# Product 4 of each column pair on the bank of products 1, 6 and 7, and a new order of the products

## The chip, the cores and the metric

The kernel runs on one NeuronCore of a Trainium2 chip. The metric is the device time of one execution in microseconds (us), the median of several runs. In the profile, PE is TensorE's matmuls, PEld its weight loads, DVE is VectorE, ACT ScalarE, POOL GpSimd, and SP the engine whose queue issues most of the DMAs. Each engine works through its own queue in order; engines wait for each other through semaphores.

## The reference

One decoder layer on a sequence of 1024 rows of width 1024. The normalized input is multiplied by one wide weight matrix, whose columns are the inputs of two kinds of heads:

```python
h = rms_norm(x, pre_g)
z = jnp.einsum('bsd,de->bse', h, w_in)          # 1024 x 1024 times 1024 x 7184
qa, ka, va, ga, qb, kb, vb, gb, gk_low = split_columns(z)
...
oa = diff_attention(qa, ka, va, lam)             # 8 heads, causal, two softmax maps each
oa = rms_norm(oa, subln_g) * (1.0 - lam_init) * silu(ga)
ob = gla_chunked(qb, kb, vb, log_a)              # 4 heads of gated linear attention
ob = rms_norm(ob, gla_g) * silu(gb)
y = jnp.einsum('bse,ed->bsd', jnp.concatenate([oa, ob], axis=-1), w_out)
return x + rms_norm(y, post_g)
```

The change lies in the projection `z = h w_in` alone.

## The kernel before, in words

**Seven products for eight.** The projection is done in 28 column pairs of 256 columns (`pairs`, lines 169 to 179). In each, the input is cut into 2 x 2 blocks of 512 x 512 (rows by depth) and the weights into 2 x 2 blocks of 512 x 128, and the four output blocks come from seven products instead of eight, by Winograd's form of Strassen's scheme. `LEFT` (line 319) names the input block of each product n; `make_weights` (line 278) makes its weight block, partly in place in the raw weights: product 5 turns b11 into b12 - b11, 6 into b22 - b12 + b11, 7 turns b12 into b22 - b12, 4 turns b21 into b21 minus what b11 now is. Each operand is split into a high part in fp32r and a rest, so that a product is three passes (high x high, rest x high, high x rest) of four matmuls of 128 x 512: twelve matmuls. The value columns VA and VB are "wide": two pairs share a weight tile, and a product has 24 matmuls of 128 x 256.

**Banks and snapshots.** A product accumulates in one of PSUM's eight banks. `step` (line 420) says which. Product 1 opens bank x; ACT copies it to SBUF as s1 (`snap`, line 424, the copy itself in line 427). Product 6 adds to the same bank x, which is copied as s2, and product 7 adds to it again, copied as s3. Product 2 opens a bank y, 5 a bank z, 4 another bank y, and 3 adds to z. The outputs are y(2) + s1, z(5) + s3, y(4) + s3 and z(5, 3) + s2. The sum of a bank and a snapshot is a DVE add (line 440, for values lines 403 and 411); `take` (line 349) and `take_values` (line 396) then split the block into high part and rest, or gate or scale it, and store it to device memory. Banks are given out in turn from the list `free` and put back in `step` once the reads from them are issued; whoever opens or adds to a bank waits for the earlier reads of it.

**The order of work.** All matmuls and transposes are pinned to the order in which the program issues them (`mm`, `tr`, lines 116 to 120). The order of the products is a list of (pair, n) written out in lines 200 to 221. Ten products stand at its head; then each pair (two pairs together where they are wide) runs 1, 2, 5, 6, 4, 7, and the third product of the pair before comes after its product 2. The last two pairs are interleaved. `go` (line 595) walks the list: it prepares the weights of the next products up to three ahead (`prepare`, in a ring of five weight buffers, `NRING`), loads the raw weights (`fetch_raw`, line 250, four buffers of 0.5 MB, two for each pair), multiplies, and does a step of converting output weights (`wo_step`, line 580: a load of 256 KB after some products, its cast to high part and rest and their stores after others, with one buffer).

Other engines' instructions are placed in their queues by a scheduler that simulates the kernel when it is built.

**Around it.** Before the products, the input is transposed and its blocks and sums are made (lines 529 to 571); decay tables for gated linear attention (GLA) are made between products (`decay`, line 680). From product 5 of pair 12 on, GLA itself runs as a filler: `go` calls `next(fill[0])` after every product, and the generator `gla` (line 758) does a block of its matmuls in some of these calls. In each half of a head, counted from 1, the 2nd call has the scores and transposes (pa, pk), the 5th the states (kv), the 7th the outputs (gpo), the 11th the norm (ms), and eleven calls make a half. The attention and the output projection follow the products.

Of the kernel before, what the change touches and what calls it, by code (L numbers as in the profile page):

```python
# [10 lines left out]
AF = mybir.ActivationFunctionType  # L11
ALU = mybir.AluOpType
PSUM = bass.MemoryType.PSUM

P = 128
# [12 lines left out]
QSCALE = 128.0 ** -0.5  # L28
# [3 lines left out]
def hymba_kernel(  # L32
# [21 lines left out]
    act, dve, pool, pe, sp = nc.scalar, nc.vector, nc.gpsimd, nc.tensor, nc.sync  # L54

    def fp(t):
        return t.bitcast(F32)
# [50 lines left out]
    free = list(range(8))  # L108
# [77 lines left out]
    def load_raw(p, halves=(0, 1)):  # L186
        if p >= len(pairs):
            return
        c0 = pairs[p][2]
        for kh in halves:  # L190
            if kh not in raws.setdefault(p, {}):
                r = ap.tile([P, HB, 256], F32, tag="raw", name="w_raw", bufs=4)
                rows = slice(kh * 512, kh * 512 + 512)
                sp.dma_start(r, w_in[0, rows, c0 : c0 + 256].rearrange("(k p) c -> p k c", p=P))
                raws[p][kh] = r
# [3 lines left out]
    EARLY = 5  # L199
    order = [(0, 1), (1, 1), (0, 2), (1, 2), (2, 1), (3, 1), (2, 2), (3, 2), (4, 1), (4, 2)]  # L200
    n_early = len(order)
    y, z = len(pairs) - 2, len(pairs) - 1
    groups = []
    for p in range(y):
        if wide(p) and p % 2:
            groups[-1].append(p)
        else:
            groups.append([p])
    for prev, group in zip([[]] + groups, groups):
        for n in (1, 2, 5, 6, 4, 7):  # L210
            if (group[0], n) not in order[:n_early]:
                order += [(p, n) for p in group]

            if n == (7 - len(group) if group[0] < EARLY else 2):
                order += [(p, 3) for p in prev]

    i = order.index((1, 4))
    order[i : i + 2] = order[i + 1], order[i]

    order += [(y, 1), (y, 2), (y - 1, 3), (y, 5), (z, 1), (z, 2), (z, 5), (y, 6), (z, 6), (y, 4)]  # L220
    order += [(y, 7), (z, 4), (z, 7), (y, 3), (z, 3)]
    LEAD = 8
    ws, ws_wide, early = {}, {}, {}

# [25 lines left out]
    def fetch_raw(p, n, i):  # L250

        if not wide(p):
            load_raw(p)
            if i >= n_early:
                load_raw(p + 1)
        elif p >= 4 or p == 0:
            load_raw(p)
            if p and n == 1:
                load_raw(p + 1)

            if n == 4:
                load_raw(p + 2, (0,))
                if p == 0:
                    load_raw(3, (0,))
            elif n == 7:
                if p == 0:
                    load_raw(3, (1,))
                else:
                    load_raw(p + 2, (1,))
        else:  # L270
            if n == 5:
                load_raw(2, (1,))
            elif n == 4:
                load_raw(4, (0,))
            elif n == 7:
                load_raw(4, (1,))

    def make_weights(i):
# [67 lines left out]

    decs = {}

    def take(kind, n, half, unit, c):

        cs = cols(half)
        if kind in ("QA", "KA"):
            h = n + unit

            ending = made[0] > len(order) - LEAD
            if ending and order[made[0] - 1][1] == 7:
                raw = ap.tile([P, 2, 512], F32R, tag="raw", name="qk_st", bufs=4)
                hi, lo = raw[:, 0], raw[:, 1]
            else:
                hi, lo = t_st("qk_hi", F32R), c.bitcast(F32R)  # L360
            scale = -0.125 if kind == "QA" else 1.0
            act.activation(hi, c, AF.Copy, scale=scale)
            dve.scalar_tensor_tensor(lo, c, scale, fp(hi), ALU.mult, ALU.subtract)
            d = qk_d["q" if kind == "QA" else "k"][h]
            for t, src in enumerate((hi, lo)):
                for m in range(2):
                    ins = sp.dma_start(d[m, t, :, cs], fp(src)[64 * m : 64 * m + 64])
                    if ending:
                        tc.keep_in_program_order(ins)
        elif kind in ("GA", "GB"):  # L370
            g = t_st("g")
            act.activation(g, c, AF.Exp, scale=-1.0)
            act.activation(g, g, AF.Ln, bias=1.0)
            act.activation(g, g, AF.Exp, scale=-1.0)
            dve.tensor_tensor(c, c, g, ALU.mult)
            d = g_d[n + unit] if kind == "GA" else gg_d[n][unit]
            sp.dma_start(d[:, cs], c)
        elif kind == "QB":
            g = n + unit
            e_q, _ = decs[g]  # L380
            qd = t_st("gqd")
            dve.scalar_tensor_tensor(c, c, QSCALE, e_q[:, cs], ALU.mult, ALU.mult)
            dve.tensor_tensor(
                qd.rearrange("p (n i) -> p n i", i=P),
                c.rearrange("p (n i) -> p n i", i=P),
                dsteps[g][:, half * 4 : half * 4 + 4].unsqueeze(2).to_broadcast([P, 4, P]),
                ALU.mult,
            )
            for t, src in enumerate((c, qd)):
                sp.dma_start(gq_d[g][t, :, cs], src)  # L390
        else:
            g = n + unit
            dve.tensor_tensor(c, c, decs[g][1][:, cs], ALU.mult)
            sp.dma_start(gq_d[g][2, :, cs], c)

    def take_values(p, half, unit, p0, p1):

        kind, n, _ = pairs[p - p % 2]
        tiles = slice(half * 4 + p % 2 * 2, half * 4 + p % 2 * 2 + 2)
        p0, p1 = (t.rearrange("p (n u c) -> p u n c", u=2, c=P) for t in (p0, p1))  # L400
        if kind == "VB":
            st = t_st("gv_st").rearrange("p (u n c) -> p u n c", u=2, c=P)
            dve.tensor_tensor(st, p0, p1, ALU.add)
            for u in range(2):
                sp.dma_start(gv_d[n + unit][u, :, tiles, :], st[:, u])
        else:
            c, hi = t_c("c"), t_st("v_hi", F32R)
            c, hi, lo = (
                t.rearrange("p (u n c) -> p u n c", u=2, c=P) for t in (c, hi, c.bitcast(F32R))
            )  # L410
            dve.tensor_tensor(c, p0, p1, ALU.add)
            act.copy(hi, c)
            dve.tensor_tensor(lo, c, fp(hi), ALU.subtract)
            for t, src in enumerate((hi, lo)):
                for u in range(2):
                    sp.dma_start(v_d[n + 2 * unit + u][t, :, tiles, :], fp(src[:, u]))
# [3 lines left out]
    def step(i):  # L420

        p, n = order[i]
        kind, m, _ = pairs[p]
        def snap(k, ps):
            other = k == "s3" and (wide(p) or p >= len(pairs) - 2)
            b[k] = t_c("s") if other else t2k("s", 4, "s")
            act.copy(b[k], ps)  # L427

        b = sums.setdefault(p, {})
        name = {1: "x", 2: "y", 5: "z", 6: "x", 4: "y", 7: "x", 3: "z"}[n]  # L430
        if n in (1, 2, 4, 5):
            b[name], b["i" + name] = take_bank([P, 512], name)
        ps = b[name]
        multiply(i, ps, n not in (6, 7, 3))

        def done(half, unit, p0, p1):
            if wide(p):
                return take_values(p, half, unit, p0, p1)
            c = t_c("c")
            dve.tensor_tensor(c, p0, p1, ALU.add)  # L440
            take(kind, m, half, unit, c)

        if n == 1:
            snap("s1", ps)
        elif n == 2:
            done(0, 0, ps, b["s1"])
            free.append(b["iy"])
        elif n == 6:
            snap("s2", ps)
        elif n == 7:  # L450
            snap("s3", ps)
            free.append(b["ix"])
            done(1, 1, b["z"], b["s3"])
            done(1, 0, b["y"], b["s3"])
            free.append(b["iy"])
        elif n == 3:
            done(0, 1, ps, b["s2"])
            free.append(b["iz"])
# [119 lines left out]
    wo_open = []  # L578

    def wo_step(n):  # L580
        if n in (1, 6) and wo_open:
            e, dh, raw = wo_open.pop()
            hi = t_c("wo_hi", F32R)
            act.copy(hi, raw)
            lo = raw.bitcast(F32R)
            dve.tensor_tensor(lo, raw, fp(hi), ALU.subtract)
            for t, src in enumerate((hi, lo)):
                sp.dma_start(wod[e][t][:, cols(dh)], fp(src))
        if n in (2, 4) and wo_todo:
            e, dh = wo_todo.pop(0)  # L590
            raw = ap.tile([P, 512], F32, tag="t4", name="wo_raw", bufs=1)
            sp.dma_start(raw, w_out[0, e * P : (e + 1) * P, cols(dh)])
            wo_open.append((e, dh, raw))
# [931 lines left out]
```

## Time and profile before

| | |
|---|---|
| time, median of 3 runs | 981.64 us (980.49 to 984.09) |
| span of the profiled execution, first to last instruction | 979.5 us |
| granted TensorE clock, mean | 0.998 |
| transposes and first products | until about 114 us |
| products, with GLA from about 270 us | until about 629 us |
| attention and output projection | from about 629 us |

The profile gives the span of its execution and no separate time for it. The lines below come from the page of that execution and from views of its trace: stretches (busy time of each engine between two times), waits (engine, line, what it waited for: us in total, times, longest), the timeline (start, duration, engine, line, operation, output from inputs, count of merged instructions, and in brackets the idle time before it and what ended it), and groups of equal instructions (count, busy time, mean in ns, idle time before). In the timeline a row of several matmuls lasts until the modelled end of the last one, which reaches into the next row, because matmuls are pipelined.

### The profile page before, as it was taken

To read this page: it belongs to the slowest core of one execution; us is meant where nothing else is said; L and a number is where in the kernel's file an instruction comes from. 1 tells how busy PE (TensorE), PEld (TensorE's weight loads), DVE (VectorE), ACT (ScalarE), POOL (GpSimd) and SP (SyncE) were. 2 spreads that over 40 slices of the span, in tenths; PEclk is the share of its full clock that TensorE was granted. 3 is DMA by queue.
4 is the path that set the end of the run, shared out by engine and by line. 5 is a ranking of instruction groups with operands and counts; after the bars stand their busy time and mean duration, and the time that the engine had idled before them with its cause. 6 is when DMAs were issued, how large, how long until landed. Compare 5 with 4: busy or idle time off the path is not lost.

```text
span 979.5 us, 15753 instructions
## 1 busy us (share of the span) xinstructions
PE 956.6 (98%) x5338; PEld 830.2 (85%) x5338; DVE 734.9 (75%) x1452; ACT 600.8 (61%) x1164; POOL 135.5 (14%) x142
## 2 busy tenths in 40 slices
PE   6999999999999999999999999999999999999997
PEld 5998988888889998899888888878888888888785
DVE  6986697798866676586786876487888888898554
ACT  8642365486367455445565775365777687887773
POOL 5200000000000010000110100021322222443321
PEclk9999999999999999999999999999999999999999
DMA  9443356747765868887987876997656769994677
GB/s 354 141 122 98 119 156 196 235 161 253 241 228 169 270 191 256 245 289 245 296 256 238 269 214 213 355 295 250 210 177 228 244 194 351 339 296 104 151 208 147
DMA packets 152593, 220.45 MB, mean 225 GB/s; under 512 B 17104, under 2 KB 83664, under 8 KB 152416
## 3 DMA queue, kind: packets, MB, share of 16 engines
q1 hardware_dynamic: 148480, 212.10, 66.2%
q0 software_dynamic: 4032, 7.34, 4.6%
q8 instruction: 42, 0.69, 0.3%
q14 instruction: 39, 0.32, 0.1%
HBM read 133.93 MB, written 88.60 MB: 227 GB/s over the span
## 4 chain that ended last, share of the span: by engine, by line
PE 87%; DMA 4%; DVE 4%; issue 1%; ACT 1%; SPq 1%; POOL 0%; DVEq 0%; ACTq 0%; POOLq 0%
PE x L117 21%; PE y L117 14%; PE z L117 14%; PE ypart L117 13%; PE sc L117 7%; PE po L117 5%; PE yps L117 4%; PE wtr L120 3%; PE gpo L117 2%; DMA w_raw<-in_w_in_dram 2%; DMA ks<-k_d 1%; PE kv L117 1%; PE gkl_ps L117 1%; DVE w L316 1%; PE pa L117 1%
## 5 line engine op out<-in xcount | busy, mean ns | idle before, releaser
L315 ACT CAST w<-w_raw 128x512 fp32r<-128x512 f32 (+1 forms) x164 | 112.3, 688 | 97.7 <-PE y L117 46.3
L316 DVE TENSOR_TENSOR w<-w_raw,w 128x512 fp32r<-128x512 f32 (+1 forms) x164 | 126.5, 774 | 50.6 <-ACT w L315 44.3
L1048 ACT ACTIVATE p<-p,stt 128x896 f32<-128x896 f32 (+7 forms) x128 | 99.3, 776 | 37.6 <-DVE stt L1038 35.8
L427 ACT COPY s<-x 128x512 f32<-128x512 f32 x84 | 49.2, 585 | 82.1 <-PE x L117 79.1
L296 DVE TENSOR_TENSOR w_raw<-w_raw 128x512 f32<-128x512 f32 (+1 forms) x96 | 75.8, 790 | 16.0 <-DMA w_raw<-in_w_in_dram 14.6
L1054 POOL TENSOR_SCALAR p<-p,stt,lam 128x1024 f32<-128x1024 f32 (+3 forms) x64 | 56.2, 878 | 226.9 <-DVE stt L1053 226.7
L1038 DVE CUSTOM_DVE_ANT_0 p<-sc,maskt 128x512 f32<-128x512 f32 (+3 forms) x128 | 74.4, 585 | 15.8 <-PE sc L117 14.2
L775 POOL TENSOR_SCALAR_AFFINE_SELECT gan<-gan 128x512 f32<-128x512 f32 x8 | 17.6, 2204 | 488.6 <-ACT gan L774 488.6
L117 PE MATMUL y<-h_hi,w 128*128 128x512 f32 x320 | 79.6, 391 | 0.0
L117 PE MATMUL z<-s_hi,w 128*128 128x512 f32 x320 | 79.6, 391 | 0.0
L117 PE MATMUL x<-s_hi,w 128*128 128x512 f32 x320 | 79.6, 391 | 0.0
L117 PE MATMUL ypart<-wo_hi,m_hi 128*128 128x512 f32 x192 | 78.8, 410 | 0.1
L117 PE MATMUL ypart<-wo_hi,m_lo 128*128 128x512 f32 x192 | 75.4, 393 | 0.0
L117 PE MATMUL ypart<-wo_lo,m_hi 128*128 128x512 f32 x192 | 75.4, 393 | 0.0
L117 PE MATMUL sc<-k,q 128*128 128x512 f32 (+1 forms) x192 | 70.4, 370 | 1.4 <-DVE stt L1038 1.2
L117 PEld LDWEIGHTS x<-s_hi,w 128*128 128x128 f32 x320 | 59.7, 188 | 12.2
L117 PEld LDWEIGHTS y<-h_hi,w 128*128 128x128 f32 x320 | 59.6, 188 | 12.2
L117 PEld LDWEIGHTS z<-s_hi,w 128*128 128x128 f32 x320 | 59.5, 188 | 12.0
L117 PE MATMUL sc<-ks,q 128*128 128x512 f32 (+1 forms) x192 | 66.4, 348 | 0.9 <-DMA ks<-k_d 0.9
L1096 ACT CAST wt_hi<-wtr 128x512 fp32r<-128x512 f32 (+1 forms) x80 | 42.8, 535 | 25.0 <-PE wtr L120 24.6
L1097 DVE TENSOR_TENSOR wt_lo<-wtr,wt_hi 128x512 fp32r<-128x512 f32 (+1 forms) x80 | 50.6, 633 | 8.3 <-ACT wt_hi L1096 7.6
L1057 DVE SCALAR_TENSOR_TENSOR p<-p,stt,p 128x1024 f32<-128x1024 f32 (+3 forms) x64 | 52.1, 814 | 4.6 <-POOL p L1054 4.4
(224 smaller groups left out, 2236.1 us busy)
## 6 DMA issues: line engine op xcount, KB each, us to landing
w_raw<-in_w_in_dram SPq DMA_DIRECT2D x56, 512.0 KB, 4.6
wo_raw<-in_w_out_dram SPq DMA_DIRECT2D x32, 256.0 KB, 3.0
wo_d<-wo_hi SPq DMA_DIRECT2D x32, 256.0 KB, 3.2
wo_d<-wo_raw SPq DMA_DIRECT2D x32, 256.0 KB, 3.6
q<-q_d SPq DMA_DIRECT2D x32, 256.0 KB, 4.8
k<-k_d SPq DMA_DIRECT2D x32, 256.0 KB, 5.6
ks<-k_d SPq DMA_DIRECT2D x64, 128.0 KB, 6.1
wo_hi<-wo_d SPq DMA_DIRECT2D x16, 512.0 KB, 6.6
```

The source lines that it names most:

```text
L117: tc.keep_in_program_order(pe.matmul(*a, **k))
L120: tc.keep_in_program_order(pe.transpose(dst, src, ident))
L296: dve.tensor_tensor(dst, a, b, ALU.subtract)
L315: act.copy(w[0], src)
L316: dve.tensor_tensor(w[1], src, fp(w[0]), ALU.subtract)
L427: act.copy(b[k], ps)
L1038: ins = dve.tensor_tensor_reduce(p[:, a:e], sc[:, : e - a], maskt[:, NZ + P - (e - a) :] if last else maskt[:, : e - a], 1.0, 3e38 if i == ...
L1048: act.activation(p[:, :n], p[:, :n], AF.Exp, bias=st[:, m : m + 1], scale=-1.0, accum_out=st[:, 2 + m : 3 + m],)
L1054: pool.tensor_scalar(p1[:, :n], p1[:, :n], st[:, 5:6], lam, ALU.mult, ALU.mult)
L1057: dve.scalar_tensor_tensor(p0[:, :n], p0[:, :n], st[:, 4:5], p1[:, :n], ALU.mult, ALU.subtract)
L1096: act.copy(hi[:, :n], pt[:, :n])
L1097: dve.tensor_tensor(lo[:, :n], pt[:, :n], fp(hi[:, :n]), ALU.subtract)
```

## The change

Product 4 now uses the bank of 1, 6 and 7: it opens no bank of its own but adds to x after the snapshot s3, so that the bank then holds the output block (1, 0) itself, and no DVE add is needed for it; `take` and `take_values` read the block from the bank. The order in each group of pairs becomes 1, 2, 5, 6, 7, 4, 3, and in a group of one pair the first product of the next group stands between 7 and 4. The raw weights and the conversion of the output weights are loaded after other products than before.

```diff
-    for prev, group in zip([[]] + groups, groups):
-        for n in (1, 2, 5, 6, 4, 7):
-            if (group[0], n) not in order[:n_early]:
-                order += [(p, n) for p in group]
-
-            if n == (7 - len(group) if group[0] < EARLY else 2):
-                order += [(p, 3) for p in prev]
-
-    i = order.index((1, 4))
-    order[i : i + 2] = order[i + 1], order[i]
-
-    order += [(y, 1), (y, 2), (y - 1, 3), (y, 5), (z, 1), (z, 2), (z, 5), (y, 6), (z, 6), (y, 4)]
-    order += [(y, 7), (z, 4), (z, 7), (y, 3), (z, 3)]
+    for group, after in zip(groups, groups[1:] + [[y]]):
+        for n in (1, 2, 5, 6, 7, 4, 3):
+            order += [(p, n) for p in group if (p, n) not in order]
+
+            if n == 7 and len(group) == 1:
+                order += [(p, 1) for p in after[:1]]
+
+    order += [(y, 2), (y, 5), (z, 1), (z, 2), (z, 5), (y, 6), (z, 6), (y, 7)]
+    order += [(z, 7), (y, 4), (z, 4), (y, 3), (z, 3)]
...
         if not wide(p):
             load_raw(p)
-            if i >= n_early:
+            if i >= n_early and n > 1:
                 load_raw(p + 1)
         elif p >= 4 or p == 0:
...
-            if n == 4:
+            if n == 7:
                 load_raw(p + 2, (0,))
+            elif n == 4:
                 if p == 0:
-                    load_raw(3, (0,))
-            elif n == 7:
-                if p == 0:
-                    load_raw(3, (1,))
+                    load_raw(3)
                 else:
                     load_raw(p + 2, (1,))
...
-    def take(kind, n, half, unit, c):
+    def take(kind, n, half, unit, src, c):
...
-            act.activation(hi, c, AF.Copy, scale=scale)
-            dve.scalar_tensor_tensor(lo, c, scale, fp(hi), ALU.mult, ALU.subtract)
+            act.activation(hi, src, AF.Copy, scale=scale)
+            dve.scalar_tensor_tensor(lo, src, scale, fp(hi), ALU.mult, ALU.subtract)
...
-            dve.tensor_tensor(st, p0, p1, ALU.add)
+            if p1 is None:
+                act.copy(st, p0)
+            else:
+                dve.tensor_tensor(st, p0, p1, ALU.add)
...
-            dve.tensor_tensor(c, p0, p1, ALU.add)
-            act.copy(hi, c)
-            dve.tensor_tensor(lo, c, fp(hi), ALU.subtract)
+            if p1 is not None:
+                dve.tensor_tensor(c, p0, p1, ALU.add)
+                p0 = c
+            act.copy(hi, p0)
+            dve.tensor_tensor(lo, p0, fp(hi), ALU.subtract)
...
-        name = {1: "x", 2: "y", 5: "z", 6: "x", 4: "y", 7: "x", 3: "z"}[n]
-        if n in (1, 2, 4, 5):
+        name = {1: "x", 2: "y", 5: "z", 6: "x", 4: "x", 7: "x", 3: "z"}[n]
+        if n in (1, 2, 5):
             b[name], b["i" + name] = take_bank([P, 512], name)
         ps = b[name]
-        multiply(i, ps, n not in (6, 7, 3))
+        multiply(i, ps, n in (1, 2, 5))
...
         elif n == 7:
             snap("s3", ps)
+            done(1, 1, b["z"], b["s3"])
+        elif n == 4:
+            done(1, 0, ps)
             free.append(b["ix"])
-            done(1, 1, b["z"], b["s3"])
-            done(1, 0, b["y"], b["s3"])
-            free.append(b["iy"])
...
     def wo_step(n):
-        if n in (1, 6) and wo_open:
+        if n in (3, 6) and wo_open:
...
-        if n in (2, 4) and wo_todo:
+        if n in (2, 7) and wo_todo:
```

What the cut leaves out: the other kinds in `take` read `src` in the same way, and pair 2 loads pair 4's raw weights after 7 and 4 instead of after 4 and 7.

More of the change, by code (lines that the diff above doesn't have):

```diff
@@ L272, in fetch_raw @@
                 load_raw(2, (1,))
+            elif n == 7:
+                load_raw(4, (0,))
             elif n == 4:
-                load_raw(4, (0,))
-            elif n == 7:
                 load_raw(4, (1,))
@@ L355, in take @@
             ending = made[0] > len(order) - LEAD
-            if ending and order[made[0] - 1][1] == 7:
+            if ending and order[made[0] - 1][1] in (7, 4):
                 raw = ap.tile([P, 2, 512], F32R, tag="raw", name="qk_st", bufs=4)
@@ L371, in take @@
             g = t_st("g")
-            act.activation(g, c, AF.Exp, scale=-1.0)
+            act.activation(g, src, AF.Exp, scale=-1.0)
             act.activation(g, g, AF.Ln, bias=1.0)
             act.activation(g, g, AF.Exp, scale=-1.0)
-            dve.tensor_tensor(c, c, g, ALU.mult)
+            dve.tensor_tensor(c, src, g, ALU.mult)
             d = g_d[n + unit] if kind == "GA" else gg_d[n][unit]
@@ L381, in take @@
             qd = t_st("gqd")
-            dve.scalar_tensor_tensor(c, c, QSCALE, e_q[:, cs], ALU.mult, ALU.mult)
+            dve.scalar_tensor_tensor(c, src, QSCALE, e_q[:, cs], ALU.mult, ALU.mult)
             dve.tensor_tensor(
@@ L392, in take, with take_values @@
             g = n + unit
-            dve.tensor_tensor(c, c, decs[g][1][:, cs], ALU.mult)
+            dve.tensor_tensor(c, src, decs[g][1][:, cs], ALU.mult)
             sp.dma_start(gq_d[g][2, :, cs], c)
-    def take_values(p, half, unit, p0, p1):
+    def take_values(p, half, unit, p0, p1=None):
         kind, n, _ = pairs[p - p % 2]
         tiles = slice(half * 4 + p % 2 * 2, half * 4 + p % 2 * 2 + 2)
-        p0, p1 = (t.rearrange("p (n u c) -> p u n c", u=2, c=P) for t in (p0, p1))
+        p0, p1 = (
+            t if t is None else t.rearrange("p (n u c) -> p u n c", u=2, c=P) for t in (p0, p1)
+        )
         if kind == "VB":
             st = t_st("gv_st").rearrange("p (u n c) -> p u n c", u=2, c=P)
-            dve.tensor_tensor(st, p0, p1, ALU.add)
+            if p1 is None:
+                act.copy(st, p0)
+            else:
+                dve.tensor_tensor(st, p0, p1, ALU.add)
             for u in range(2):
@@ L429, in step, with done @@
         b = sums.setdefault(p, {})
-        name = {1: "x", 2: "y", 5: "z", 6: "x", 4: "y", 7: "x", 3: "z"}[n]
-        if n in (1, 2, 4, 5):
+        name = {1: "x", 2: "y", 5: "z", 6: "x", 4: "x", 7: "x", 3: "z"}[n]
+        if n in (1, 2, 5):
             b[name], b["i" + name] = take_bank([P, 512], name)
         ps = b[name]
-        multiply(i, ps, n not in (6, 7, 3))
-        def done(half, unit, p0, p1):
+        multiply(i, ps, n in (1, 2, 5))
+        def done(half, unit, p0, p1=None):
             if wide(p):
@@ L439, in done @@
             c = t_c("c")
-            dve.tensor_tensor(c, p0, p1, ALU.add)
-            take(kind, m, half, unit, c)
+            if p1 is not None:
+                dve.tensor_tensor(c, p0, p1, ALU.add)
+                p0 = c
+            take(kind, m, half, unit, p0, c)
         if n == 1:
```

## The prediction, made before the changed kernel was run

> **What bounds the kernel now.** I read the page's engine rows first, then the busy time of each engine in stretches of the projection stage, then the list of what TensorE (PE) waited for, then single pairs in the timeline.
>
> ```profile
> span 979.5 us, 15753 instructions
> PE 956.6 (98%) x5338; PEld 830.2 (85%) x5338; DVE 734.9 (75%) x1452; ACT 600.8 (61%) x1164; POOL 135.5 (14%) x142
> ...
> PEclk9999999999999999999999999999999999999999
> ...
> PE 87%; DMA 4%; DVE 4%; issue 1%; ACT 1%; SPq 1%; POOL 0%; DVEq 0%; ACTq 0%; POOLq 0%
> ```
>
> ```profile
> 114.00:267.00 153.00, 153.00 (x699) 127.68 (x698) 128.25 (x211) 89.31 (x152) 0.00 (x0) 1.00 0.63 203
> ...
> 372.00:467.00 95.00, 93.13 (x629) 85.99 (x628) 64.17 (x95) 48.29 (x83) 2.11 (x2) 1.00 0.83 260
> 467.00:593.00 126.00, 126.00 (x642) 107.29 (x641) 95.11 (x154) 81.25 (x148) 10.04 (x3) 1.00 0.81 255
> ```
>
> ```profile
> PE xT L120 <- DVE x L482: 8.6, 4, 7.2
> PE gpo L117 <- DVE gu L803: 1.9, 1, 1.9
> PE y L117 <- DVE s L565: 1.3, 1, 1.3
> PE sc L117 <- DVE stt L1038: 1.2, 2, 0.9
> ...
> PE y L117 <- ACT s L427: 0.7, 1, 0.7
> ```
>
> The columns of the stretches are length, then busy time of PE, weight load, DVE, ACT and POOL. PE is busy for all 153 us of the first and all 126 us of the last stretch at clock 1.00, and the whole list of PE's waits holds only three between the transposes at the start and the attention (1.9, 1.3 and 0.7). So in this stage the end is set by PE alone: work taken from DVE or ACT gains nothing, and every microsecond by which PE is made to wait is added to the time.
>
> **The steady pattern.** Pair 5 shows what lies between the sixth product and the next use of its bank:
>
> ```profile
> 139.91 1.98 PE L117 MATMUL x<-s_hi,w 128*128 128x512 f32 x8
> ...
> 141.72 1.07 PE L117 MATMUL x<-s_lo,w 128*128 128x512 f32 x4
> ...
> 142.63 1.98 PE L117 MATMUL y<-h_hi,w 128*128 128x512 f32 x8
> 142.83 0.59 ACT L427 COPY s<-x 128x512 f32<-128x512 f32 x1 [2.10 <-PE x L117]
> ...
> 145.35 1.98 PE L117 MATMUL x<-s_hi,w 128*128 128x512 f32 x8
> ```
>
> Product 6 issues from 139.91 and product 4 follows at 142.63, so a product takes 2.72 us. Product 6's last result is there at 141.72 + 1.07 = 142.79, ACT copies the bank (s2) from 142.83 to 143.42, and product 7 writes to that bank again at 145.35. The copy is hidden by product 4.
>
> **Part 1: 6 and 7 become neighbours.** The new order in a single pair is 1, 2, 5, 6, 7, next 1, 4, 3. Product 7 accumulates on the bank from which the s2 copy (line 427, called in line 449) must first have read the state after 6, and the matmuls are pinned to this order, so PE has nothing to do in between. The next pair's first product stands between 7 and 4; nothing stands between 6 and 7. The trace of before has this very wait once, where a product needs the bank that has just been copied:
>
> ```profile
> 65.68 2.08 PE L117 MATMUL x<-w,s_hi 128*128 128x256 f32 x16
> ...
> 67.60 1.12 PE L117 MATMUL x<-w,s_lo 128*128 128x256 f32 x8
> ...
> 68.76 0.59 ACT L427 COPY s<-x 128x512 f32<-128x512 f32 x1 [1.15 <-PE x L117]
> ...
> 69.40 2.18 PE L117 MATMUL y<-w,h_hi 128*128 128x256 f32 x16 [0.68 <-ACT s L427]
> ...
> 72.38 0.88 PE L117 MATMUL x<-w,s_hi 128*128 128x256 f32 x6
> ```
>
> There 16 matmuls take 67.60 - 65.68 = 1.92 us, so a wide product takes 2.88. The next should have begun at 68.56 and the one after it at 71.44; they began at 69.40 and 72.38. The wait cost 0.94 us in all: 0.84 until the first matmul and 0.10 in its refill. For the narrow form it is the same from pair 5: the copy ends at 143.42 against an unhindered start at 142.63, and the same 0.05 from copy to matmul and 0.10 of refill make 0.94. I take 0.94, with 0.84 as the lower bound.
>
> How often: pairs 4 to 25 without the four wide ones (14, 15, 18, 19) are 18 single pairs. Pairs 26 and 27 run interleaved (y6, z6, y7, z7) and have cover. The wide groups run 6, 6, 7, 7 and have it too. Counting the steps of the gated-linear-attention (GLA) filler from product 5 of pair 12, its score block (eight matmuls pa, four transposes pk) falls behind product 6 of pairs 12 and 23 and covers them:
>
> ```profile
> 539.27 1.07 PE L117 MATMUL x<-s_lo,w 128*128 128x512 f32 x4
> 540.18 1.05 PE L117 MATMUL pa<-kq 128*128 128x128 f32 x8
> ...
> 541.43 2.10 PE L117 MATMUL y<-h_hi,w 128*128 128x512 f32 x8
> ```
>
> That block takes 1.25 us, more than 0.94. Sixteen pairs stay bare: 16 x 0.94 = **15.0 us**.
>
> [...]
>
> **Part 2: a late ACT now counts.** So far a copy s2 that started late was free as long as product 4 ran. Mostly it is not late (pair 5: 0.04 us after the bank was full), but of the sixteen pairs three were late by over half a microsecond:
>
> ```profile
> 116.45 1.07 PE L117 MATMUL x<-s_lo,w 128*128 128x512 f32 x4
> 118.31 0.57 ACT L427 COPY s<-x 128x512 f32<-128x512 f32 x1
> 374.08 1.07 PE L117 MATMUL x<-s_lo,w 128*128 128x512 f32 x4
> 376.70 0.57 ACT L427 COPY s<-x 128x512 f32<-128x512 f32 x1
> 516.62 1.07 PE L117 MATMUL x<-s_lo,w 128*128 128x512 f32 x4
> 521.39 0.62 ACT L584 CAST wo_hi<-wo_raw 128x512 fp32r<-128x512 f32 x1 [7.57 <-DMA wo_raw<-in_w_out_dram]
> 521.91 0.58 ACT L427 COPY s<-x 128x512 f32<-128x512 f32 x1
> ```
>
> The banks were full at 117.52, 375.15 and 517.69; the copies began 0.79, 1.55 and 4.22 us later, 6.6 us together. In the last one ACT stood 7.57 us at a cast of output weights whose load had not landed, with the copy queued behind it. Whether the new schedule puts such casts before the copy the trace of before cannot show. Between nothing (no copy late) and twice the sum (13.2) I take the sum found, **6.6 us**, since the same engine serves the same work. The output-weight step moves from products 1 and 6 (loads at 2 and 4) to 3 and 6 (loads at 2 and 7); its load at 2 now has products 5 and 6 before its cast instead of 3, 5 and 6, 5.4 us instead of 8.2, which pushes to the upper side.
>
> **Part 3: product 4 on the bank of 1, 6, 7.** It removes one add of the other bank and s3 in every single pair and every VA pair (20 + 4), turns four in the VB pairs into an ACT copy, and frees one bank of four per pair.
>
> ```profile
> L440 DVE TENSOR_TENSOR c<-y,s 128x512 f32<-128x512 f32 x39 | 26.7, 683 | 6.0 <-PE y L117 4.3 <-ACT s L427 1.6
> L316 DVE TENSOR_TENSOR w<-w_raw,w 128x1024 fp32r<-128x1024 f32 x16 | 19.5, 1220 | 6.0 <-PE x L117 2.7 <-issue 1.9 <-PE z L117 1.1
> ```
>
> 24 x 0.683 = 16.4 us leave DVE, whose 128 of 153 us lie beside a PE that is always busy: 0 on the path. The casts that followed the add now read PSUM in its place; they are as many as before. Product 4 must wait for the copy s3, but the next pair's product 1 (2.72 us) lies over its 0.04 + 0.59 + 0.05, and a lateness up to 2.0 us is free there. Product 3 waits for the reading of z, two products behind 7 as before. At the start the wait of 0.94 us shown above disappears, since product 4 no longer takes a new bank there: **-0.9 us**, and nothing is late next, because 4 of pair 0 stands two wide products behind 6 and one behind 7.
>
> **Part 4: weights and loads.** Where a single pair stands before a wide group (13 before 14, 17 before 18), the wide product 1 holds two of the five weight buffers past products 4 and 3; handed out in turn, the second weight buffer of wide product 2 comes free only when the second wide product 1 ends. Its subtraction takes 1.22 us against eight matmuls of 0.12 that can go first: 2 x (1.22 + 0.04 - 0.96) = **0.6 us**, between 0 (buffers taken in another order) and 2.4 (no cover). The load of the next pair's raw weights moves from the preparation of product 1 to that of product 2:
>
> ```profile
> w_raw<-in_w_in_dram SPq DMA_DIRECT2D x56, 512.0 KB, 4.6
> ...
> wo_raw<-in_w_out_dram SPq DMA_DIRECT2D x32, 256.0 KB, 3.0
> ```
>
> It lands in 4.6 us after its issue, and its first use is prepared four products (10.9 us) later: 0. It stays in SP's queue behind stores of results that are as many as before. The one wait of 1.9 us (gpo for gu, in the stretch from 372) may go or come elsewhere as the filler's blocks fall behind other products: 0, with 1.9 either way. The attention stage is unchanged.
>
> **Sum.** 15.0 + 6.6 - 0.9 + 0.6 = +21.3 us on the span of 979.5. The three times of before have the median 981.64, 2.1 above that span; I carry this over: 981.64 + 21.3 = **1003**.
>
> **Rivals.**
> (a) ACT is always in time, the filler's wait goes, the refill costs nothing: 16 x 0.84 - 0.9 - 1.9 = +10.6, 992. For it: most copies of before start at once. Against it: the three rows above.
> (b) ACT's queue becomes the bound between 6 and 7: if half of the sixteen copies wait as long as the last two late ones did on average ((1.55 + 4.22) / 2 = 2.9), 8 x 2.9 = 23 us stand for 6.6, and 1020 comes out. The shorter lead of the output-weight load speaks for it; the stretches with 89 of 153 and 81 of 126 us of ACT work speak against.
> (c) The clock falls. Sixteen gaps of about a microsecond, each followed by one product at half rate, would cost 16 x 2.72 = 43.5 us more: 1046. Against it:
>
> ```profile
> 0.00:25.00 25.00, 15.80 (x96) 13.99 (x97) 16.86 (x36) 21.50 (x44) 12.88 (x21) 1.00 0.99 356
> ```
>
> The first 25 us have four PE waits of 8.6 us together and the clock 1.00. [...]
> (d) Not slower: the end of product 6 and the copy are hidden after all, because something else stands between 6 and 7. The place is each bare pair, the price 0.94, and it decides when at least 15 of the 16 are covered and the copies are in time; then -0.9 is left, and at best also the filler's wait (-1.9), the early one for DVE (-1.3) and that of the first scores for DVE (-1.2): 976.3 to 981. The freed 16.4 us of DVE work speaks for it; the pinned order of the matmuls and the list of products speak against it.
> (e) The change doesn't do what it says, and product 7 is not behind 6 on PE: then the time stays at 982.
>
> **Chances.** Forecast 0.80, its own range 994 to 1011; (a) 0.06; (b) 0.05; (c) 0.02; (d) 0.04; (e) 0.03. The range 991 to 1012 holds the forecast and (a) and leaves out the rest. About 0.5% (4.9 us) is what a measurement of this kernel can tell from no change: faster than that is the far end of (d), 0.02; within it are (e) and the rest of (d), 0.05; slower 0.93.
>
> **What would show it.** In the list of PE's waits after, a new group of PE x (or its weight load) waiting for ACT s L427, some 16 times, 0.7 to 0.8 us each by that view's count, sum 11 to 20; in the timeline of a single pair, product 7 starting 3.6 us after 6; PE's busy time unchanged and the stretches of the projection no longer full. Part 2 is right if a few of these waits are over 1.5 us with another ACT instruction just before the copy; wrong if none or most are. Part 3 is right if the wait at 69 us is gone and DVE's busy time falls by 14 to 20 us. The prediction is wrong if that group has fewer than ten waits, or if another group is longer.

## The result, and the profile after

The changed kernel takes 1020.43 us (median of 4 runs, 1017.43 to 1021.14) against 981.21 us for the kernel before: a ratio of 1.0381, 95% interval 1.0361 to 1.0402. It is slower, as forecast, but by 39 us where 21 were forecast, and outside the range of 991 to 1012. The profiled execution took 1017.43 us, its span is 1015.7 us, 36.2 more than the span before. The sums below are made on these two spans; the median run took 3.0 us more than the profiled one, which no trace shows. In the timelines, rows of other engines and tiles between two lines are left out also where no dots stand.

The page of the changed kernel:

```profile
span 1015.7 us, 15723 instructions
...
PE 968.7 (95%) x5338; PEld 834.0 (82%) x5338; DVE 720.4 (71%) x1424; ACT 606.6 (60%) x1168; POOL 130.5 (13%) x142
...
PE 77%; DMA 7%; DVE 6%; ACT 5%; issue 2%; SPq 1%; POOL 0%; DVEq 0%; ACTq 0%; POOLq 0%
```

PE's share of the chain that ended last has fallen by 10 points, and DMA, DVE and ACT have taken its place. PE's busy time has risen by 12.1 us although its 5338 matmuls are the same ones: some of them ran more slowly, as shown below. DVE's has fallen by 14.5. The list of PE's waits and two stretches of the projection:

```profile
PE x L117 <- ACT s L429: 26.3, 18, 4.7
PE xT L120 <- DVE x L486: 9.1, 4, 7.2
...
PE y L117 <- DVE s L569: 1.3, 1, 1.3
```

```profile
114.00:267.00 153.00, 142.44 (x622) 115.89 (x621) 113.05 (x184) 82.91 (x141) 0.00 (x0) 0.98 0.53 171
267.00:372.00 105.00, 97.03 (x567) 85.68 (x566) 59.27 (x86) 52.01 (x86) 1.49 (x2) 0.95 0.62 204
```

There is one new group: PE waits 18 times, 26.3 us in all and up to 4.7 us at a time, for the copy of line 429 (`snap`, line 427 before). The stretches are no longer full, and the granted clock, the number behind the last count in brackets, is 0.98 in the first stretch where it was 1.00, and 0.95 in the second (0.989 over the span, 0.998 before). The waits for gpo (1.9) and at 69 us (0.7) are gone from the list.

A single pair whose copy is in time, pair 6:

```profile
164.12 1.98 PE L117 MATMUL x<-s_hi,w 128*128 128x512 f32 x8
...
165.93 1.07 PE L117 MATMUL x<-s_lo,w 128*128 128x512 f32 x4
167.03 0.59 ACT L429 COPY s<-x 128x512 f32<-128x512 f32 x1 [2.04 <-PE x L117]
...
167.67 2.11 PE L117 MATMUL x<-s_hi,w 128*128 128x512 f32 x8 [0.68 <-ACT s L429]
169.62 1.07 PE L117 MATMUL x<-s_lo,w 128*128 128x512 f32 x4
170.53 1.75 PE L117 MATMUL x<-h_hi,w 128*128 128x512 f32 x7
```

Product 7 starts 3.55 us behind 6, and the two take 170.53 - 164.12 = 6.41 us where two products take 5.44: the bare neighbour costs 0.97 us, of which the list of waits counts 0.68; the other 0.29 is the end of product 6 (0.15: it ends at 166.99, 7 could have started at 166.84) and the refill (0.14: product 7 takes 170.53 - 167.67 = 2.86 us instead of 2.72).

A pair whose copy is late, pair 11:

```profile
273.06 1.07 PE L117 MATMUL x<-s_lo,w 128*128 128x512 f32 x4
274.35 0.33 SPq L596 DMA_DIRECT2D wo_raw<-in_w_out_dram  x1
277.69 0.62 ACT L588 CAST wo_hi<-wo_raw 128x512 fp32r<-128x512 f32 x1 [5.56 <-DMA wo_raw<-in_w_out_dram]
278.21 0.58 ACT L429 COPY s<-x 128x512 f32<-128x512 f32 x1
...
278.84 3.78 PE L117 MATMUL x<-s_hi,w 128*128 128x512 f32 x8 [4.71 <-ACT s L429]
```

The bank is full at 274.13. But ACT's next instruction is the cast of output weights whose load SP issued only at 274.35; ACT stands at it for 5.56 us, the copy is queued behind, and PE waits 4.71. Eight matmuls then take 3.78 us instead of the 2.11 of pair 6.

In pairs 12 and 23 the score block of GLA stands between 6 and 7, as the prediction counted, so sixteen places are bare. But there the copy is late by more than the block lasts. Pair 12:

```profile
299.49 1.07 PE L117 MATMUL x<-s_lo,w 128*128 128x512 f32 x4
300.40 1.05 PE L117 MATMUL pa<-kq 128*128 128x128 f32 x8
301.29 0.60 PE L120 MATMUL pk<-ident,kq 128*128 128x128 f32 x4
303.31 0.62 ACT L588 CAST wo_hi<-wo_raw 128x512 fp32r<-128x512 f32 x1 [4.29 <-DMA wo_raw<-in_w_out_dram]
303.84 0.58 ACT L429 COPY s<-x 128x512 f32<-128x512 f32 x1
304.47 3.65 PE L117 MATMUL x<-s_hi,w 128*128 128x512 f32 x8 [2.58 <-ACT s L429]
```

Its wait of 2.58 us, and the 1.45 of pair 23, are lateness alone. The end of the block and the refill come on top: in pair 23 the two products and the block take 8.50 us, 1.81 more than 5.44 + 1.25.

Why eight matmuls take longer after some waits, the stretches of the same kernel in which the clock is down show:

```profile
147.40:150.80 3.40, 3.40 (x10) 2.61 (x9) 2.91 (x9) 0.59 (x1) 0.00 (x0) 0.50 0.73 205
232.70:236.10 3.40, 3.09 (x7) 2.51 (x8) 2.79 (x4) 1.73 (x3) 0.00 (x0) 0.51 0.83 311
277.10:283.90 6.80, 5.06 (x12) 4.00 (x13) 1.39 (x2) 1.62 (x3) 0.00 (x0) 0.50 0.58 203
304.40:307.80 3.40, 3.33 (x8) 2.65 (x9) 0.95 (x2) 1.51 (x4) 0.66 (x1) 0.50 0.95 313
...
sum 17.00, PE 14.88 PEld 11.77 DVE 8.03 ACT 5.46 POOL 0.66; mean PE 3.72 PEld 2.94 DVE 2.01 ACT 1.36 POOL 0.16
```

Four times, during a long wait, at its end or (pair 5) 1.4 us after it, the granted clock goes to half for one or two periods of 3.4 us. PE works 14.88 us in them, half of which, 7.4 us, is lost. These 7.4 us and 16 x 0.29 = 4.6 us at the bare places make up the rise of PE's busy time.

So the 36.2 us of the span come apart like this:

| | us |
|---|---|
| 16 places where nothing stands between 6 and 7, 0.97 each | +15.5 |
| late copies, waits: 26.3 - 16 x 0.68 = 15.4; the rest in pairs 12 and 23, about 0.35 each: 0.7 | +16.1 |
| half clock after long waits | +7.4 |
| the wait at 69 us gone | -0.9 |
| the wait for gpo gone | -1.9 |
| sum | 36.2 |

The small waits elsewhere in the list, 13.7 us together against 13.3 before, are left out, so that the sum comes out to a tenth is partly chance.

### The profile page after: what moved, and what is told of

Read it like the earlier page. It is cut to its first block, busy times and chain, and to the rows that moved or that the text cites. A ratio compares the mean times of both kernels' runs of the same rounds, so it can differ in the third digit from the quotient of the medians.

```text
span 1015.7 us, 15723 instructions
## 1 busy us (share of the span) xinstructions
PE 968.7 (95%) x5338; PEld 834.0 (82%) x5338; DVE 720.4 (71%) x1424; ACT 606.6 (60%) x1168; POOL 130.5 (13%) x142
## 4 chain that ended last, share of the span: by engine, by line
PE 77%; DMA 7%; DVE 6%; ACT 5%; issue 2%; SPq 1%; POOL 0%; DVEq 0%; ACTq 0%; POOLq 0%
PE x L117 25%; PE ypart L117 12%; PE z L117 11%; PE sc L117 7%; PE po L117 5%; PE y L117 5%; PE yps L117 4%; PE wtr L120 3%; DMA wo_d<-wo_raw 3%; DMA wo_raw<-in_w_out_dram 3%; PE gpo L117 2%; ACT s L429 1%; PE kv L117 1%; DVE w L310 1%; PE gkl_ps L117 1%
## 5 line engine op out<-in xcount | busy, mean ns | idle before, releaser
L117 PE MATMUL x<-s_hi,w 128*128 128x512 f32 x320 | 87.0, 417 | 26.3 <-ACT s L429 26.3
L117 PEld LDWEIGHTS x<-s_hi,w 128*128 128x128 f32 x320 | 61.8, 199 | 45.9 <-ACT s L429 33.5
L1042 DVE CUSTOM_DVE_ANT_0 p<-sc,maskt 128x512 f32<-128x512 f32 (+3 forms) x128 | 74.3, 585 | 14.7 <-PE sc L117 13.2
L779 POOL TENSOR_SCALAR_AFFINE_SELECT gan<-gan 128x512 f32<-128x512 f32 x8 | 12.8, 1596 | 523.8 <-ACT gan L778 523.8
L117 PE MATMUL x<-h_hi,w 128*128 128x512 f32 x320 | 79.8, 391 | 0.0
L117 PEld LDWEIGHTS x<-h_hi,w 128*128 128x128 f32 x320 | 60.2, 190 | 12.5
L443 DVE TENSOR_TENSOR c<-z,s 128x512 f32<-128x512 f32 x40 | 27.5, 688 | 51.0 <-ACT s L429 36.1
```

The lines of the kernel that those rows point to most:

```text
L117: tc.keep_in_program_order(pe.matmul(*a, **k))
L1042: ins = dve.tensor_tensor_reduce(p[:, a:e], sc[:, : e - a], maskt[:, NZ + P - (e - a) :] if last else maskt[:, : e - a], 1.0, 3e38 if i == ...
```

## The experiments

The theory after the result: the order alone is the loss (7 behind 6 on one bank); casts of output weights that ACT has ahead of the copy make it worse; and long waits bring the clock down. Rivals: the shared bank costs something itself; the loads are late in any order; the clock went down for another reason. The medians of the kernel before beside these runs were 981.64, 981.41 and 981.14 us for the three sets.

**The cast behind the copy.** The changed kernel; `snapped[0]` is the last copy that `snap` made.

```diff
-            act.copy(hi, raw)
+            with tc.issue_after(snapped[0]) if n == 6 else nullcontext():
+                act.copy(hi, raw)
```

> Only the cast of output weights after product 6 is held behind the copy s2 in ACT's queue. Theory (in the changed kernel the copy is late because that cast waits for its load in front of it, and the long waits then halve the clock for a while): 18 waits of PE x for ACT s stay, 0.68 us each where nothing else is late, sum about 14 us instead of 26.3, none over 2 us; granted clock 0.997 or more; time 1020.4 - 12.4 (late copies) - 6 (clock) = 1002, 998 to 1006. Rival (the loads are late in any order, and PE then waits for something else): 1015 to 1022 with a new group of PE waits.

Measured: 1002.45 us, ratio 1.0218 (1.0196 to 1.0240). Its waits, and pair 11 again:

```profile
PE x L117 <- ACT s L430: 15.2, 17, 2.1
```

```profile
267.60 1.07 PE L117 MATMUL x<-s_lo,w 128*128 128x512 f32 x4
268.70 0.59 ACT L430 COPY s<-x 128x512 f32<-128x512 f32 x1 [2.04 <-PE x L117]
268.86 0.33 SPq L598 DMA_DIRECT2D wo_raw<-in_w_out_dram  x1
269.34 2.11 PE L117 MATMUL x<-s_hi,w 128*128 128x512 f32 x8 [0.68 <-ACT s L430]
...
272.18 0.62 ACT L590 CAST wo_hi<-wo_raw 128x512 fp32r<-128x512 f32 x1 [2.89 <-DMA wo_raw<-in_w_out_dram]
```

The load is issued as late as before, 0.19 us after the bank was full, but the cast now waits behind the copy and nobody needs it. The waits of late copies fall from 15.4 to 15.2 - 16 x 0.68 = 4.3 us, the granted clock is 0.999 (0.995 and 0.996 in the other runs of this kernel, 0.988 to 0.990 in those of the changed one), and 18 us are gone. The sum of waits was 15.2, not 14, and one wait was 2.1 (pair 23, where ACT still had a gate and a cast of GLA ahead); in pair 12 the score block of GLA covered everything. The edge is put on this cast alone, so it was the cast that made most of the copies late, and without the longest waits the clock stayed up, fully in the profiled run and mostly in the others. The theory holds; the loads being late is not the loss, the queue position is.

**Product 5 between 6 and 7.**

```diff
-        for n in (1, 2, 5, 6, 7, 4, 3):
+        for n in (1, 2, 5, 6, 7, 4, 3) if len(group) > 1 else (1, 2, 6, 5, 7, 4, 3):
...
+        if order[i][1] == 6 and (order[i][0], 5) in order[i + 1 :]:
+            prepare(i + 1)
```

The second edit makes the weights of 5 first, because those of 6 are built from them in place.

> In single pairs product 5 goes between 6 and 7 (1, 2, 6, 5, 7, next 1, 4, 3); the bank of product 4 stays shared. Theory (the loss is only that 7 follows 6 on one bank): no wait of PE x for ACT s over 0.3 us, clock 0.998, time 978 to 983. Rival (adding four products on one bank costs time in itself, or the loads do): over 990.

Measured: 982.22 us, ratio 1.0009 (0.9998 to 1.0020), clock 0.998. Waits and pair 6:

```profile
PE x L117 <- ACT s L431: 1.6, 2, 1.2
```

```profile
157.78 1.98 PE L117 MATMUL x<-s_hi,w 128*128 128x512 f32 x8
...
160.50 1.98 PE L117 MATMUL z<-s_hi,w 128*128 128x512 f32 x8
160.70 0.59 ACT L431 COPY s<-x 128x512 f32<-128x512 f32 x1 [1.58 <-PE x L117]
...
163.22 1.98 PE L117 MATMUL x<-s_hi,w 128*128 128x512 f32 x8
```

Four products still share a bank, one bank less is used and 24 DVE adds are missing, and the time is that of the kernel before. So the shared bank costs and brings nothing that can be measured here (at most 0.2%): the adds removed lay beside a busy PE (151.81 of the 153 us from 114 to 267). Against the expectation two waits of over 0.3 us are left (1.2 and 0.4), both copies queued behind other ACT work.

**A bank of its own in the new order.**

```diff
-        name = {1: "x", 2: "y", 5: "z", 6: "x", 4: "x", 7: "x", 3: "z"}[n]
-        if n in (1, 2, 5):
+        name = {1: "x", 2: "y", 5: "z", 6: "x", 4: "y", 7: "x", 3: "z"}[n]
+        if n in (1, 2, 4, 5):
...
-        multiply(i, ps, n in (1, 2, 5))
+        multiply(i, ps, n in (1, 2, 4, 5))
...
             snap("s3", ps)
+            free.append(b["ix"])
             done(1, 1, b["z"], b["s3"])
         elif n == 4:
-            done(1, 0, ps)
-            free.append(b["ix"])
+            done(1, 0, ps, b["s3"])
+            free.append(b["iy"])
```

> The new order with product 4 on a bank of its own and the DVE add with s3 as before the change. Theory (the order is the loss, the shared bank costs nothing): the same 18 waits, 1012 to 1030. Rival (the shared bank is the loss): 978 to 990.

Measured: 1021.94 us, ratio 1.0411 (1.0376 to 1.0447), clock 0.985, with

```profile
PE x L117 <- ACT s L429: 27.2, 17, 3.7
```

The loss is all there without the shared bank: the new order makes it, with the new places of the loads and of the conversion that came with it. With the experiment before, both halves of the change are told apart.

**A second bare place.** The next pair's product 1 goes behind 4.

```diff
-            if n == 7 and len(group) == 1:
+            if n == 4 and len(group) == 1:
```

> The next pair's first product goes behind 4 instead of between 7 and 4, so single pairs have a second place where a product follows on the bank just copied. Theory (each such place costs about 0.97 us, plus late copies): 18 more waits, 1020.4 + 17.5 = 1038, with late copies up to 1050. Rival (ACT's backlog is the bound, and a second stop only gives it time): 1020 to 1028.

Measured: 1041.35 us, ratio 1.0611 (1.0576 to 1.0646).

```profile
PE x L117 <- ACT s L429: 40.2, 36, 4.9
```

18 more waits and 20.9 us more than the changed kernel; 18 x 0.97 is 17.5 of it, and the other 3.4 were not followed up.

**Two and five more copies.** The kernel with the cast behind the copy, with more copies of the bank into the same tile ahead of s2 in the 18 single pairs (two here, five in the other).

```diff
+            for _ in range(2 if k == "s2" and n_single(p) else 0):
+                act.copy(b[k], ps)
             snapped[:] = [act.copy(b[k], ps).ins]
```

> The kernel with the cast behind the copy, and in front of each copy s2 of the 18 single pairs two more copies of the same bank (0.48 us each). Theory (a late copy adds to the time one for one, and only long stops lower the clock): stops of about 1.6 us, 1002.5 + 18 x 0.96 = 1020 with the clock at 0.998, up to 1028 where some stops halve it for a while. Rival (ACT catches up elsewhere and the delay is partly hidden): under 1012.

> As with two more copies, but five: stops of about 3.1 us. One for one without the clock: 1002.5 + 18 x 2.4 = 1046. Theory (stops of over about 2 us lower the clock to half for 3.4 us in most cases, at a price of some 1.5 us each): 1060 to 1080 and a granted clock of 0.97 to 0.98. Rival (the clock went down in the changed kernel for another reason): 1046 with 0.995 or more.

Measured: 1051.22 us with two (ratio 1.0708, 1.0690 to 1.0727; clock 0.975) and 1108.71 us with five (one run; clock 0.949). Waits with two and with five:

```profile
PE x L117 <- ACT s L435: 44.2, 18, 3.6
```

```profile
PE x L117 <- ACT s L435: 82.2, 18, 7.7
```

Both went past their range, because the added copies hold the last one back by more than taken: in pair 6 the three copies last from 173.16 to 175.37,

```profile
173.16 0.59 ACT L434 COPY s<-x 128x512 f32<-128x512 f32 x1 [2.04 <-PE x L117]
173.64 0.62 ACT L309 CAST w<-w_raw 128x512 fp32r<-128x512 f32 x1
174.16 0.59 ACT L434 COPY s<-x 128x512 f32<-128x512 f32 x1
174.78 0.59 ACT L435 COPY s<-x 128x512 f32<-128x512 f32 x1
175.42 1.90 PE L117 MATMUL x<-s_hi,w 128*128 128x512 f32 x7 [2.30 <-ACT s L435]
```

so the last one starts 1.62 us after the first: a cast of weights stands between the first two (0.52), and the third follows the second after 0.62, not after the 0.48 that lie between the first copy and that cast. The waits rose by 44.2 - 15.2 = 29.0 and by 67.0 us, the times by 48.8 and 106.3. The difference, 19.8 and 39.3 us, goes with a clock that is 0.975 and 0.949 where it was 0.999: PE is busy for 49.3 and 86.4 us at half clock, half of which is 24.6 and 43.2, somewhat more than the difference. So a late copy counts about one for one, and long waits cost once more through the clock.

**The kernel before with 7 ahead of 4 in single pairs.**

```diff
-        for n in (1, 2, 5, 6, 4, 7):
+        for n in (1, 2, 5, 6, 4, 7) if len(group) > 1 else (1, 2, 5, 6, 7, 4):
```

Not shown in the diff: the output block of 4 is then taken after 4 instead of after 7.

> The kernel before, with only product 7 moved ahead of 4 in the single pairs (the bank of 4, the place of product 3 and the conversion of output weights stay; pair 4 has cover by the third products of pairs 2 and 3). Theory (the neighbours cost 0.97 us each, the late copies come from the new places of the output weights): 17 stops, 981.6 + 16.5 + 6 = 1004, 998 to 1010, with late copies as few as before. Rival (the neighbours themselves make the copies late): 1015 to 1025.

Measured: 1003.50 us, ratio 1.0240 (1.0214 to 1.0267), clock 0.993.

```profile
PE x L117 <- ACT s L427: 15.8, 15, 2.9
```

15 waits, since the score block covers pairs 12 and 23 here, which the expectation had forgotten. The waits of late copies are 15.8 - 15 x 0.68 = 5.6 us, close to the 6.6 of the trace of before. Two of the waits, 2.9 and 2.7 us, brought the clock to half, for 10.2 us in which PE was busy for 9.5; so 1003.5 holds 4.8 us of clock that the 1004 expected did not have. With the old places of product 3, of the loads and of the conversion the copies are late less often; this run does not tell which of the three does it.

**A longer lead for the cast at 6, and the same with 5 between.** The changed kernel, and the one with 5 between 6 and 7.

```diff
-        if n in (3, 6) and wo_open:
+        if n in (4, 6) and wo_open:
...
-        if n in (2, 7) and wo_todo:
+        if n in (3, 7) and wo_todo:
```

> The changed kernel with the conversion of output weights shifted by one product: casts after 4 and 6 instead of 3 and 6, loads after 3 and 7 instead of 2 and 7, so that four products instead of three lie between the cast before and the cast at 6. Theory (the cast at 6 comes too early for its load, whose one buffer has first to be stored and filled, and holds the copy s2 back): late copies fall from 14 us to 3 to 8, few halvings of the clock, 1001 to 1010. Rival (the place of the conversion does not matter, the bare neighbours make ACT late): 1015 to 1022.

> Product 5 between 6 and 7 and the conversion of output weights after 4 and 6 with loads after 3 and 7. Theory: as with product 5 between, less the wait of 1.2 us in which product 4 stood behind a cast at 3 whose load was late: 980 to 982, no measurable difference from the kernel before. Rival (the conversion then collides elsewhere): 983 to 986.

Measured: 1014.47 us (ratio 1.0344, 1.0326 to 1.0362; clock 0.991) and 987.58 us (1.0066, 1.0049 to 1.0082). Both expectations missed: the first time lies just below the rival's range, the second above both ranges. Waits of the first and of the second:

```profile
PE x L117 <- ACT s L429: 23.4, 16, 4.5
```

```profile
PE x L117 <- ACT s L431: 6.2, 6, 3.3
```

The waits of late copies were still 23.4 - 16 x 0.68 = 12.5 us. So the lead of the load is not what matters most. What goes with the late copies is a count over the traces: of the 18 copies s2 in single pairs, those ahead of which a cast of output weights ended only after the bank was full. There are 2 before, 3 with 7 ahead of 4 in the kernel before, 7 in the changed kernel, 8 with a bank of its own, 8 here, and 0 with the cast held behind. Why the scheduler puts the cast ahead so often in the new order stays open.

**Both casts behind the copies, with 5 between.** As in the first experiment but for the casts at 3 and 6, on the kernel with 5 between.

> Product 5 between 6 and 7, and the casts of output weights held behind the last copy of a bank in ACT's queue. Theory: the two waits of PE x for ACT s that are left with product 5 between (1.2 and 0.4 us) are late copies behind such a cast or a gate; the 1.2 goes: 980 to 981.5, at best just below the kernel before. Rival (the casts come later and their stores and loads delay the weights): 983 to 988.

Measured: 983.83 us, ratio 1.0026 (1.0012 to 1.0039), PE x waiting for ACT s 2.0 us. The waits did not go, and the time is the rival's; why was not followed up. No version here beats the kernel before.

## Why the prediction was right and wrong

Right: PE alone sets the end in this stage; the new order leaves 7 behind 6 bare; sixteen places are bare, and one costs 0.94 (measured 0.97: 15.5 us where 15.0 were forecast); the DVE adds bring nothing though DVE's work falls by 14.5 us; the wait at 69 us goes; 3.6 us between 6 and 7; the late copies have another ACT instruction just ahead, and six of the waits are over 1.5 us. Two of its signs did not come: the new group's sum is 26.3, not 11 to 20, and PE's busy time rose.

Wrong in size, and two terms make it:

- **Part 2, "I take the sum found, 6.6 us, since the same engine serves the same work".** It measured 16.1. Lateness is no property of the engine but of its queue: of the nine late copies of the changed kernel, seven had a cast of output weights ahead of them that ended only after the bank was full, against two of eighteen before, and with this cast held back the late copies cost 4.3. The text named the move of the casts and let it push only on the range. It also left pair 23 out as covered, though its own trace had a copy there that began 2.64 us after the bank was full at 540.34, behind such a cast, and the block covers 1.25:

```profile
542.45 0.62 ACT L584 CAST wo_hi<-wo_raw 128x512 fp32r<-128x512 f32 x1 [0.76 <-DMA g_d<-c]
542.98 0.58 ACT L427 COPY s<-x 128x512 f32<-128x512 f32 x1
```

  That moving the conversion is what puts the casts there is not shown: the longer lead changed little, and the kernel before with 7 ahead of 4 (5.6) keeps more than the conversion in its old place. Its 1003.5 meets the forecast of 1003 partly by luck, since 4.8 us of it are clock. Rival (b) is nearest to what happened, half of the copies late behind ACT's queue, but its 1020 (its own terms give 1019.3) is met by luck too: it had 23 us for late copies and none for the clock, where the runs have 16.1 and 7.4.
- **Rival (c), the clock, at 0.02.** The clock, taken at nothing in the sum, measured 7.4 us, not after each wait as the rival had it but after four long ones. The row it was dismissed with says nothing of the clock. In the trace of before, the first product, in that very stretch of 25 us with the clock column at 1.00, looks like this:

```profile
13.63 4.11 PE L117 MATMUL x<-w,h_hi 128*128 128x256 f32 x16 [0.60 <-ACT h_hi L521]
```

Sixteen matmuls of this size took 1.92 us at 65.68. Here the matmuls behind them start 3.94 us later (17.57), so they ran at half rate, and the column still shows 1.00: it cannot be read there, and the durations of equal matmuls had to be compared.

Smaller: the wait for gpo left with the new places of the filler (-1.9, taken as 0). The wait for the weight buffers ahead of wide groups (0.6) does not appear in the list. The range was too short on the upper side because both terms were bounded by the trace of an order in which late copies were harmless: twice the sum found, 13.2, was taken as the most for late copies, and nothing for the clock.

## What to carry to other kernels

Before moving work away from between two uses of one accumulator, count what hid its evacuation: here 0.97 us a time on the engine that sets the end, against adds removed from an engine that did not. An instruction that becomes critical must be looked at in its queue: what is ahead of it, and what that waits for, since the late copies (16.1 us) cost as much as the bare places themselves (15.5). If the queue cannot be avoided, hold the other work behind the copy by an explicit edge; where another product already covers the copy, as with 5 between, the edge brought nothing (983.83 us with it, 982.22 without).

## What the hardware showed that was not expected

In these runs the TensorE clock went to half at waits of less than 2 us too, and the length of the wait alone did not decide it. In the profiled run of the changed kernel it went down to 0.50 during or after waits of 1.86 (pair 5), 3.33, 4.71 and 2.58 us, for 3.4 us or twice that, and not after one of 1.91 (pair 7) or 2.25 (pair 21):

```profile
146.02 2.62 PE L117 MATMUL x<-s_hi,w 128*128 128x512 f32 x8 [1.86 <-ACT s L429]
...
188.92 2.11 PE L117 MATMUL x<-s_hi,w 128*128 128x512 f32 x8 [1.91 <-ACT s L429]
```

After the second the eight matmuls take the usual 2.11. In the profiled run of the kernel with the cast behind the copy none of the 17 waits brought the clock down (1.00 in every stretch from 114 to 629), the longest of them 2.1; in the one with the longer lead a wait of 1.79 did (pair 5) and one of 2.82 did not (pair 8). What else decides it no run shows.
